# Products on 64 rows by turns between the two halves of the array, and selection operands filled up to 128 rows

## The chip, the cores and the metric

The kernel runs on one core of a Trainium2 chip, in one launch. The time is that of the device in microseconds, from launch to end; a comparison rests on the median of several runs. The profile is of one execution.

## The reference

A small language model with several kinds of layers is applied to one sequence of 256 tokens with 1024 channels, all in float32. Eleven stages follow each other: an RWKV-7 mixer, a gate with a per-layer embedding, differential attention, a second such gate, a norm, a feed-forward block, a Mamba-2 mixer (state space), two feed-forward blocks, sliding-window attention, and a last feed-forward block. Three of them contract over 64 elements only, and one over 64 selected rows:

```
# RWKV-7, 16 heads of 64, per token
sa    = einsum('bhij,bhj->bhi', state, kk_t)
state = state * w_t - sa b_t + v_t k_t ;  y_t = einsum('bhij,bhj->bhi', state, r_t)
...
# differential attention, 8 heads with two maps of 64 each
s   = einsum('bhcqd,bhckd->bhcqk', qi, kt) * scale        # c: the two maps
att = softmax(s)[:, :, 0] - lam * softmax(s)[:, :, 1]
...
# Mamba-2, 32 heads in 4 groups
seg    = acum[:, :, None] - acum[:, None, :]
scores = cb[..., None] * exp(where(causal, seg, -inf))
...
# sliding-window attention, 16 heads of 64 with 2 key heads
p = softmax(q k^T / 8 + bias, with a sink)
```

## The kernel before, in words

Tokens are held as two tiles of 128. Every product with weights is made of three products in a rounded float32 format (an upper and a lower part of each operand, the lower by lower one left out): `wload` fetches 512 KB of a weight matrix through SP's queue into `wr`, ScalarE makes the upper part `wh`, VectorE the lower part `wl`, and the sums stand in the long PSUM buffers `pl` (four banks). Everything else on TensorE writes into the short PSUM buffers `ps` (four banks; `pm`, `pq` and `pt` are one and the same).

Each stage is written as Python generators. `weave` runs them by turns, one step up to each `yield`; that order is the priority with which a scheduler then places the instructions on the engines, by its own estimate of when each is ready. `late` fixes an instruction behind what its engine was given earlier.

In the RWKV stage the 16 heads are four groups of four. A group runs through projections (`pre`), then for each of two chunks of 128 tokens through `scores` and `solve`, then `post`; the four groups start some turns after each other, and gate projections and others fill in between. `scores(t, g)` transposes the rows of two heads at a time, so that one head of a pair lies on partitions 0 to 63 and the other on 64 to 127 (`E_`). For each of the four heads it then takes one `ps` buffer, makes two products over 64 rows (128 x 256 each, plain float32, which the trace shows as two records each), and multiplies the result with a mask in two VectorE operations, into `GB` and `GK`. A `yield` follows each head. The inverse of a triangle (six levels of small float16 products, each into a `ps` buffer) and the delta rule come after it.

In differential attention `head(hd)` makes for each of its two maps one `ps` buffer with two products over 64 rows (128 x 128 and 128 x 256), then the softmax of this map, then a `yield`. Two chains of heads run beside each other. In sliding-window attention `front(pr)` does the same for the two heads of a pair.

In the state-space stage `heads(g)` needs, for each of 8 heads, the cumulated decays of that head on every partition. They come by a product of a selection matrix `sel` (64 rows, 8 x 128 columns) with the transposed decays `aT` (64 rows by 384 used columns; rows 32 to 63 hold the lower parts), in the rounded float32 format, one record each. Two small bfloat16 products add the causal mask. `sel` is a new tile for each of the four groups, with one buffer; two VectorE copies fill it. Before that, `aT` is written by one ScalarE and two VectorE operations.

Of the kernel before, what the change touches and what calls it, by code (L numbers as in the profile page):

```python
# [18 lines left out]
P = 128  # L19
D = 1024  # L20
NEG = -1.0e30
NREF = 1  # refinements of the triangular solve
# banks of PSUM for short and for long use
# [12 lines left out]
# columns of the constant block  # L36
# [3 lines left out]
def constants():  # L40
    """Masks, the identity, rotary angles and distance buckets: from the shapes alone."""
# [18 lines left out]
    # reversed distance vector: column m holds the distance 255 - m; row 32 the mask outside the window  # L60
# [14 lines left out]
def weave(*gens):  # L75
    """Trace the generators by turns, a step each."""
    gens = list(gens)
    while gens:
        for g in list(gens):
            try:  # L80
                next(g)
            except StopIteration:
                gens.remove(g)
# [13 lines left out]
def par(*gens):  # L97
    """The generators by turns, as one generator."""
    gens = list(gens)
    while gens:  # L100
        for g in list(gens):
            try:
                next(g)
            except StopIteration:
                gens.remove(g)
        yield


def spread(n, m, gen):
    """The generator's n steps over m turns."""  # L110
    at = 0
    for i in range(m):
        while at * m < (i + 1) * n:
            at += 1
            if next(gen, gen) is gen:
                return
        yield
    yield from gen


def spaced(n, *gens):
    """The generators one after another, n turns between."""
    for g in gens:
        yield from g
        for _ in range(n):
            yield


def when(cond, gen):
    """The generator, from the step on at which its condition holds."""  # L130
    while not cond():
        yield
    yield from gen
# [8 lines left out]
class Net:  # L142
# [27 lines left out]
    def m(self, shape, dt=F32, tag="m", bufs=24):  # L170
        """Small tiles: those without a tag outlive a stage, the others do not."""
        pool = self.mp if tag in ("m", "ecc", "bon", "junk") else self.st
        return pool.tile(list(shape), dt, tag=tag, name=self.nm(tag), bufs=bufs)
# [43 lines left out]
    def masked(self, out, a, b, least, init=3.0e38):  # L217
        """out = -(a + b), and its least element, not above init."""
        self.V.tensor_tensor_reduce(out=out, in0=a, in1=b, scale=-1.0, scalar=init, op0=ALU.add, op1=ALU.min,
                                    accum_out=least)  # L220
# [10 lines left out]
    def rsqrt(self, out, a, scale, eps):  # L231
        """out = (a * scale + eps) ** -0.5"""
# [4 lines left out]
    def bc(self, vec, n):  # L237
        """A DRAM vector on every partition."""
# [7 lines left out]
    def late(self, ins):  # L246
        """Not before what its engine was given earlier: for loads and constants that need not be early."""
        self.tc.keep_in_program_order(ins)

# [1 line left out]
    def prologue(self, cst):  # L251
# [10 lines left out]
        # short vectors, on every partition  # L262
# [11 lines left out]
    def first_cols(self, names, queue):  # L274
        """Per-channel vectors, channels onto partitions."""
# [16 lines left out]
    def load_x(self, tile, early=False):  # L292
        """The input, as the residual so far."""
# [18 lines left out]
    def more_cols(self):  # L312
# [14 lines left out]
        # the gain of the final norm and of the first feed-forward norm after it  # L327
# [9 lines left out]
    def wload(self, W, k0, kn, n0, nn):  # L337
        """[128, kn, nn] of W as an upper and a lower part that sum to it exactly."""
# [37 lines left out]
    def linear_cm_g(self, xT, K, W, n0, nn, evac):  # L376
        """The product with channels on partitions: evac takes two tiles of 128 channels by 256 tokens."""
# [16 lines left out]
    def linear2_g(self, xT, K, W, n0, evac):  # L394
        """256 columns, both token tiles side by side."""
# [22 lines left out]
    def split_g(self, src, ks, gains, outs):  # L418
        """src(t, k): [128 tokens, 128 channels]; appends channel-major pairs per gain."""
# [32 lines left out]
    def rstd(self):  # L452
        """Per-token 1/rms of the residual, [128, 2]."""
# [8 lines left out]
    def begin(self, gains):  # L462
        """The stage's input: per-token 1/rms and the residual, channel-major, times each gain."""
# [5 lines left out]
    def finish(self, l0, l1, gains):  # L469
        """The residual's two halves, and the next stage's input on the way."""  # L470
# [33 lines left out]
    def ffn(self, i, j, nxt, kv=False):  # L504
# [7 lines left out]
        def row():  # L512
            """1/rms as a row, on every partition."""
# [39 lines left out]
    def ple_proj(self, i):  # L553
        """p @ w_proj, kept in DRAM until its gate is known."""
# [35 lines left out]
    def final_norm(self):  # L590
        """The residual becomes its norm; what follows takes the operand from before it, the norm's
        gain and per-token factor folded in."""
# [13 lines left out]
    def rwkv(self, nxt):  # L606
        """The mixer up to its output projection: groups of four heads follow each other through
        projections, scores, triangular inverse, delta rule and group norm."""
# [22 lines left out]
        # normed input and its difference to the token before, channels on partitions  # L631
# [38 lines left out]
        def lora():  # L670
            """First stage of the low-rank decay (partitions 0-63) and in-context rate (64-127)."""
# [15 lines left out]
        def value(g):  # L687
            """Values less their mean over the head: the rule keeps the columns apart, so its output
            comes out centred as well."""
# [22 lines left out]
        def pre(g):  # L712
            """Decay and in-context rate, then keys and receptances, scaled by the running decay."""
# [68 lines left out]
        def scores(t, g):  # L782
            """One chunk of 128 tokens: products of the scaled rows, and the inverse (transposed,
            rounded) of the unit triangle that the delta rule solves with."""
# [11 lines left out]
            for hd in range(4):  # L796
                e, pr = E_(hd), hd // 2
                ps = self.pq()
                x = o[e, pr].rearrange("p a b -> p (a b)")
                self.mm(ps[:, 0:256], bk[e, pr, 0], x)  # L800
                self.mm(ps[:, 256:512], bk[e, pr, 1], x)
                for d, at in ((G, 0), (Gk, 256)):
                    self.mul(d[:, :, hd], t2(ps[:, at:at + 256]), mask)
# [43 lines left out]
        def solve(t, g):  # L847
            """The four heads' delta rule over the chunk, with the state before it and the state after."""
# [61 lines left out]
        def post(g):  # L910
            """Group norm (of rows centred already), bonus, gate."""
# [30 lines left out]
        def residual():  # L942
            """Loaded once the scan is well under way."""
# [13 lines left out]
    def diff(self, nxt):  # L957
# [5 lines left out]
        # lambda, on every partition  # L963
# [6 lines left out]
        self.stt(nlam[:], ls[:, 1:2], -LAM0, ls[:, 0:1], ALU.add, ALU.subtract)  # -(lambda)  # L970
        sub_row = self.vec["da_subln"]
        # rotary tables with the norm (and, for queries, the scale) folded in
# [47 lines left out]
        # the causal mask, after columns without one  # L1020
# [4 lines left out]
        def head(hd):  # L1025
# [3 lines left out]
            for c in range(2):  # L1029
                rs = slice(c * 64, c * 64 + 64)  # L1030
                ps = self.pq()
                self.mm(ps[:, 0:P], qT[rs, 0:P], kT[rs, 0:P])
                self.mm(ps[:, P:384], qT[rs, P:256], kT[rs, :])
# [53 lines left out]
    def ssm(self, nxt):  # L1087
# [6 lines left out]
        def conv(c0, ps, out):  # L1094
            """ps: two channel tiles [128, 2, 256]; twice the silu of the convolution into out."""
# [13 lines left out]
        def proj_cm(n0, done):  # L1109
            """512 columns; their convolution with channels on partitions."""  # L1110
# [17 lines left out]
        # step sizes: softplus(v) = max(v, 0) + 2 atanh(e / (2 + e)), e = exp(-|v|)  # L1128
# [10 lines left out]
        def steps():  # L1139
            # channels 0-31: with the weights' upper part, 32-63: with their lower part  # L1140
# [37 lines left out]
        # decays, twice side by side  # L1178
# [17 lines left out]
        aT = self.m([64, 512], F32R, "aT", 1)  # L1196
        self.act(aT[:, 0:256], pb[:64, 0:256])
        self.sub(aT[32:64, 0:256], pb[32:64, 0:256], aT[32:64, 0:256].bitcast(F32))
        self.V.tensor_copy(aT[:, 256:384], aT[:, 128:256].bitcast(F32))
        # 0.5 dt for the halves left out of the silu  # L1200
# [33 lines left out]
        def heads(g):  # L1234
# [5 lines left out]
            sel = self.m([64, 8, P], F32R, "sel", 1)  # L1240
# [40 lines left out]
        def piece(w):  # L1281
            """A piece of the work beside the heads, by its name."""
# [21 lines left out]
    def shared_kv(self, r, x):  # L1304
        I = self.I
        self.kT, self.kv, vv = {}, {}, self.s()
        kn = self.m([P, 64], tag="kn", bufs=1)  # the keys' gain, and the queries'
# [28 lines left out]
    def bias_vec(self):  # L1336
        """Per head, the bias against the distance (and the mask outside the window), to DRAM."""
# [12 lines left out]
    def swa(self, nxt):  # L1350
# [14 lines left out]
        def qproj(f):  # L1365
            qq, pss, ss = {}, [], self.m([P, 2, 8])

            def ev(t, ps):
                # with r inside the root: 1/8 of r rsqrt(r^2 sum / 64 + eps)
# [28 lines left out]
        def front(pr):  # L1398
            """Both heads' exponentials, and what divides them."""
            kv = pr // 4  # L1400
            for e_ in range(2):
                hd, rs = pr * 2 + e_, slice(e_ * 64, e_ * 64 + 64)
                ps = self.pq()
                self.mm(ps[:, 0:P], qT[pr][rs, 0:P], self.kT[rs, kv, 0:P])
                self.mm(ps[:, P:384], qT[pr][rs, P:256], self.kT[rs, kv, :])
# [64 lines left out]
    def gains(self, stage):  # L1470
        """Gains that the stage's input is taken with."""
# [80 lines left out]
```

## Time and profile before

| what | value |
|---|---|
| median of 3 runs | 1572.88 us (1570.53 to 1576.21) |
| span of the profiled execution, first to last instruction | 1568.3 us |
| own time of the profiled execution | not listed apart from the three runs; the median lies 4.6 us above the span |
| TensorE busy | 1525.5 us, 97% of the span |
| VectorE, ScalarE, GpSimd busy | 1065.5, 815.9, 77.5 us |
| mean granted TensorE clock | 0.997 of full speed |
| read from memory, written | 242.16 MB, 6.29 MB |

Instructions are counted as busy from start to modelled end, and TensorE's overlap; the distance from one start to the next start tells more of what one occupies. "s" and "ps" are names of tiles, `pl<-wh,s` means that `pl` is written from `wh` and `s`; `64*128` after MATMUL is rows by columns of the array, and `64x256` the operand that streams through. L226 is the helper `mm` and L197 the helper `tt`, so tiles tell where an instruction belongs: `qr,bk` are the scores of RWKV, `aT,sel` the selection, and `s,s` with 64 rows the attention maps and heads.

### The profile page before, as it was taken

How to read it: one execution, taken by the hardware profiler on the slowest of the kernel's cores; microseconds unless marked ns; L12 is line 12 of the kernel's file. 1: busy time of each engine (PE TensorE's matmuls, PEld its weight loads, DVE VectorE, ACT ScalarE, POOL GpSimd, SP SyncE). 2: the span in 40 equal slices, each digit the busy share in tenths (PEclk: the TensorE clock that was granted, in tenths of full speed). 3: DMA queues.
4: the chain of work that ended last, by engine and by line, in shares of the span. 5: the costliest groups of instructions: out<-in, count | busy, mean ns of one | idle time of the engine just before them, and what ended most of it. 6: DMA issues, size and time to landing. Idle time of an engine off the chain costs nothing.

```text
span 1568.3 us, 25792 instructions
## 1 busy us (share of the span) xinstructions
PE 1525.5 (97%) x10164; PEld 1349.5 (86%) x10164; DVE 1065.5 (68%) x1796; ACT 815.9 (52%) x1374; POOL 77.5 (5%) x79
## 2 busy tenths in 40 slices
PE   4999999999899999999999999999999999999998
PEld 4988988777678999887777899998999987799987
DVE  6887777876587756559877756665665657666563
ACT  3546546554466544447666744444544445654342
POOL 0000001111200000000000000000000002000000
PEclk9999999999999999999999999999999999999999
DMA  7421224566946554664442555465554653255463
GB/s 206 139 78 57 73 78 145 181 203 156 248 137 202 181 194 135 229 190 136 121 121 95 178 174 193 154 230 172 165 192 157 229 189 119 85 185 166 159 213 107
DMA packets 145500, 249.88 MB, mean 159 GB/s; under 512 B 11161, under 2 KB 42921, under 8 KB 145380
## 3 DMA queue, kind: packets, MB, share of 16 engines
q1 hardware_dynamic: 138420, 233.87, 46.4%
q0 software_dynamic: 3200, 10.81, 3.3%
q10 hardware_dynamic: 3760, 3.58, 0.9%
q8 instruction: 79, 1.29, 0.3%
q14 instruction: 41, 0.34, 0.1%
HBM read 242.16 MB, written 6.29 MB: 158 GB/s over the span
## 4 chain that ended last, share of the span: by engine, by line
PE 90%; DVE 4%; DMA 2%; ACT 2%; POOL 1%; issue 1%; ACTq 0%; POOLq 0%; DVEq 0%
PE pl L226 73%; PE ps L226 13%; PE ps L229 3%; DMA wr<-in_da_w_in_dram 1%; DVE wl L197 1%; DVE s L197 1%; DMA wa<-in_rw_w_dram 1%; DVE ac L209 1%; ACT s L223 0%; POOL s L993 0%; DVE s L209 0%; POOL m L234 0%; ACT h L223 0%; DMA wr<-in_rw_w_in_dram 0%; DMA base<-in_constants_dram 0%
## 5 line engine op out<-in xcount | busy, mean ns | idle before, releaser
L226 PE MATMUL pl<-wh,s 128*128 128x512 f32 (+1 forms) x2336 | 681.2, 370 | 6.2 <-ACT wh L223 3.2
L197 DVE TENSOR_TENSOR wl<-wr,wh 128x1024 fp32r<-128x1024 f32 (+1 forms) x460 | 528.5, 1173 | 123.0 <-ACT wh L223 121.7
L223 ACT ACTIVATE wh<-wr 128x1024 fp32r<-128x1024 f32 (+1 forms) x460 | 451.1, 1012 | 171.8 <-PE pl L226 103.3
L226 PE MATMUL pl<-s,wh 128*128 128x256 f32 x2816 | 509.1, 283 | 0.0
L226 PEld LDWEIGHTS pl<-wh,s 128*128 128x128 f32 x2336 | 422.3, 189 | 77.8 <-ACT wh L223 6.4
L226 PEld LDWEIGHTS pl<-s,wh 128*128 128x128 f32 x2816 | 439.5, 192 | 0.2
L226 PE MATMUL pl<-wl,s 128*128 128x512 f32 (+1 forms) x1168 | 430.2, 369 | 2.1 <-DVE wl L197 2.1
L226 PE MATMUL pl<-s,wl 128*128 128x256 f32 x1408 | 398.5, 283 | 0.0
L226 PEld LDWEIGHTS pl<-s,wl 128*128 128x128 f32 x1408 | 270.2, 192 | 0.0
L226 PEld LDWEIGHTS pl<-wl,s 128*128 128x128 f32 x1168 | 221.5, 190 | 36.0 <-DVE wl L197 3.3
L223 ACT ACTIVATE s<-s 128x512 f32<-128x512 f32 (+2 forms) x97 | 61.0, 629 | 209.7 <-DVE s L197 209.7
L197 DVE TENSOR_TENSOR s<-pl,s 128x512 f32<-128x512 f32 x44 | 30.4, 691 | 93.7 <-PE pl L226 93.7
L197 DVE TENSOR_TENSOR s<-pl,R 128x512 f32<-128x512 f32 x44 | 30.3, 691 | 82.8 <-PE pl L226 82.6
L234 POOL TENSOR_TENSOR m<-m,base 128x2 f32<-128x2 f32 (+2 forms) x25 | 24.2, 970 | 1006.9 <-DVE m L215 1006.9
L223 ACT ACTIVATE h<-ps 128x512 f16<-128x512 f32 x88 | 48.1, 600 | 36.9 <-PE ps L226 36.8
L223 ACT ACTIVATE s<-ps,base 128x256 fp32r<-128x256 f32 (+1 forms) x104 | 45.7, 471 | 25.0 <-PE ps L229 16.2
L209 DVE SCALAR_TENSOR_TENSOR s<-ps,base,s 128x256 fp32r<-128x256 f32 x96 | 43.6, 479 | 7.2 <-ACT s L223 6.1
L223 ACT ACTIVATE junk<-H 128x512 bf16<-128x512 f32 x40 | 25.1, 627 | 43.6 <-DVE H L209 29.2
L209 DVE SCALAR_TENSOR_TENSOR s<-s,s 128x512 f32<-128x512 f32 x56 | 38.4, 685 | 10.1 <-ACT s L223 9.4
L209 DVE SCALAR_TENSOR_TENSOR H<-pl,m,H 128x512 f32<-128x512 f32 x16 | 12.0, 751 | 47.1 <-PE pl L226 47.1
L226 PE MATMUL ps<-h,h 128*128 128x128 f16 x544 | 42.7, 220 | 1.3 <-ACT h L223 1.2
L226 PEld LDWEIGHTS <-h 128*128 128x128 f16 x576 | 34.9, 99 | 8.4 <-issue 4.8
(229 smaller groups left out, 1324.9 us busy)
## 6 DMA issues: line engine op xcount, KB each, us to landing
wr<-in_ffn_w_dram SPq DMA_DIRECT2D x248, 512.0 KB, 4.6
wr<-in_ssm_w_in_dram SPq DMA_DIRECT2D x40, 512.0 KB, 4.5
wr<-in_rw_w_in_dram SPq DMA_DIRECT2D x32, 512.0 KB, 4.7
wr<-in_da_w_in_dram SPq DMA_DIRECT2D x32, 512.0 KB, 4.7
wr<-in_pe_w_gate_dram SPq DMA_DIRECT2D x16, 512.0 KB, 4.3
wr<-in_ffn_w_dram SPq DMA_DIRECT2D x32, 256.0 KB, 3.1
wr<-in_ssm_w_out_dram SPq DMA_DIRECT2D x16, 512.0 KB, 3.8
wr<-in_rw_w_out_dram SPq DMA_DIRECT2D x8, 512.0 KB, 6.6
```

What stands on the lines that cost most here:

```text
L197: self.V.tensor_tensor(out=out, in0=a, in1=b, op=op)
L209: self.V.scalar_tensor_tensor(out=out, in0=a, scalar=sc, in1=b, op0=op0, op1=op1, **k)
L223: self.A.activation(out, a, f, **k)
L226: self.T.matmul(out, l, r, start=start, stop=stop)
L229: self.T.transpose(out, a, self.ident)
L234: self.G.tensor_tensor(out=out, in0=out, in1=self.mhalf[:, :out.free_size()].rearrange("p (a b) -> p a b", a=out.shape[1]) if len(out.shap ...
```

## The change

In `scores` the two heads of a pair are taken together: two `ps` buffers are taken at once, and the four products are issued by turns, first operand on partitions 0 to 63, then on 64 to 127, then the second operand of each. A `yield` follows, and then the four masks. The number of turns is the same. In `head` of differential attention and `front` of sliding-window attention both maps, or both heads, take their buffers together, and the products alternate between the halves in the same way; the softmax parts then follow one after the other as before. In the state-space stage `aT` and `sel` have 128 rows; rows 64 to 127 are set to zero once by two VectorE memsets in program order, and `sel` is one tile for all four groups. All other lines of the diff are comments.

```diff
-            for hd in range(4):
-                e, pr = E_(hd), hd // 2
-                ps = self.pq()
-                x = o[e, pr].rearrange("p a b -> p (a b)")
-                self.mm(ps[:, 0:256], bk[e, pr, 0], x)
-                self.mm(ps[:, 256:512], bk[e, pr, 1], x)
-                for d, at in ((G, 0), (Gk, 256)):
-                    self.mul(d[:, :, hd], t2(ps[:, at:at + 256]), mask)
+            for pr in range(2):
+
+                two = [self.pq(), self.pq()]
+                for a in range(2):
+                    for e, ps in enumerate(two):
+                        q = E_(e)
+                        self.mm(ps[:, a * 256:(a + 1) * 256], bk[q, pr, a], o[q, pr].rearrange("p a b -> p (a b)"))
+                yield
+                for e, ps in enumerate(two):
+                    for d, at in ((G, 0), (Gk, 256)):
+                        self.mul(d[:, :, pr * 2 + e], t2(ps[:, at:at + 256]), mask)
                 yield
...
-            for c in range(2):
-                rs = slice(c * 64, c * 64 + 64)
-                ps = self.pq()
-                self.mm(ps[:, 0:P], qT[rs, 0:P], kT[rs, 0:P])
-                self.mm(ps[:, P:384], qT[rs, P:256], kT[rs, :])
+            two = [self.pq(), self.pq()]
+            for q, ks in ((slice(0, P), slice(0, P)), (slice(P, 256), slice(0, 256))):
+                for c, ps in enumerate(two):
+                    rs = slice(c * 64, c * 64 + 64)
+                    self.mm(ps[:, q.start:q.start + ks.stop], qT[rs, q], kT[rs, ks])
+            for c, ps in enumerate(two):
                 S = e()
...
-        aT = self.m([64, 512], F32R, "aT", 1)
-        self.act(aT[:, 0:256], pb[:64, 0:256])
+
+        aT = self.m([P, 512], F32R, "aT", 1)
+        sel = self.m([P, 8, P], F32R, "sel", 1)
+        self.late(self.V.memset(aT[64:P, 0:384].bitcast(F32), 0.0))
+        self.late(self.V.memset(sel[64:P].bitcast(F32), 0.0))
+        self.act(aT[:64, 0:256], pb[:64, 0:256])
         self.sub(aT[32:64, 0:256], pb[32:64, 0:256], aT[32:64, 0:256].bitcast(F32))
-        self.V.tensor_copy(aT[:, 256:384], aT[:, 128:256].bitcast(F32))
+        self.V.tensor_copy(aT[:64, 256:384], aT[:64, 128:256].bitcast(F32))
...
-            sel = self.m([64, 8, P], F32R, "sel", 1)
...
-            for e_ in range(2):
-                hd, rs = pr * 2 + e_, slice(e_ * 64, e_ * 64 + 64)
-                ps = self.pq()
-                self.mm(ps[:, 0:P], qT[pr][rs, 0:P], self.kT[rs, kv, 0:P])
-                self.mm(ps[:, P:384], qT[pr][rs, P:256], self.kT[rs, kv, :])
+            two = [self.pq(), self.pq()]
+            for q, ks in ((slice(0, P), slice(0, P)), (slice(P, 256), slice(0, 256))):
+                for e_, ps in enumerate(two):
+                    rs = slice(e_ * 64, e_ * 64 + 64)
+                    self.mm(ps[:, q.start:q.start + ks.stop], qT[pr][rs, q], self.kT[rs, kv, ks])
+            for e_, ps in enumerate(two):
+                hd = pr * 2 + e_
                 S = e()
```

## Rows read from the trace of the kernel before

**Rows 1.** Page, the chain that ended last, shares by engine

```profile
PE 90%; DVE 4%; DMA 2%; ACT 2%; POOL 1%; issue 1%; ACTq 0%; POOLq 0%; DVEq 0%
```

**Rows 2.** Busy time by stretch: stretch, length, then each engine (instructions), clock, DMA

```profile
core 0: us, PE busy (x) PEld busy (x) DVE busy (x) ACT busy (x) POOL busy (x), PEclk, DMA share, GB/s
87.00:250.00 163.00, 161.67 (x1392) 140.86 (x1391) 125.76 (x240) 84.21 (x149) 10.21 (x7) 1.00 0.26 79
190.00:215.00 25.00, 25.00 (x218) 22.34 (x215) 23.07 (x44) 12.26 (x21) 0.00 (x0) 1.00 0.21 65
...
740.00:860.00 120.00, 119.09 (x660) 92.42 (x659) 96.56 (x167) 77.90 (x157) 4.44 (x4) 1.00 0.38 116
```

**Rows 3.** Waits of TensorE, 87 to 250: total us, times, longest

```profile
PE ps L226 <- DVE h L197: 0.7, 1, 0.7
```

**Rows 4.** TensorE's products by form: busy us, mean ns, idle before

```profile
L226 PE MATMUL ps<-qr,bk 64*128 64x256 f32 x128 | 33.7, 401 | 0.1
...
L226 PE MATMUL ps<-aT,sel 64*128 64x384 f32 x32 | 14.1, 440 | 0.0
```

**Rows 5.** Timeline of TensorE around one head's scores: start, length, what

```profile
98.14 1.13 PE L226 MATMUL ps<-qr,bk 64*128 64x256 f32 x4
99.19 0.38 PE L226 MATMUL pl<-wh,s 128*128 128x256 f32 x1
```

**Rows 6.** Timeline of TensorE, the scores of the first chunk

```profile
87.12 2.10 PE L226 MATMUL ps<-qr,bk 64*128 64x256 f32 x16
89.15 0.33 PE L229 MATMUL ps<-base,b 128*128 128x128 f32 x1
```

**Rows 7.** Timeline of TensorE, sliding window

```profile
1318.12 0.40 PE L226 MATMUL pl<-wh,s 128*128 128x512 f32 x1
1318.45 0.93 PE L226 MATMUL ps<-s,s 64*128 64x128 f32 x8
1319.31 0.50 PE L226 MATMUL pl<-wh,s 128*128 128x512 f32 x1
...
1319.88 0.40 PE L226 MATMUL pl<-wh,s 128*128 128x512 f32 x1
1320.20 0.92 PE L226 MATMUL ps<-s,s 64*128 64x128 f32 x4
1321.05 0.50 PE L226 MATMUL pl<-wh,s 128*128 128x512 f32 x1
```

**Rows 8.** Timeline of TensorE at full height (520 us) and around a selection (792 us)

```profile
520.00 0.28 PE L226 MATMUL pl<-s,wl 128*128 128x256 f32 x1
520.12 0.40 PE L226 MATMUL pl<-s,wh 128*128 128x256 f32 x2
...
791.88 0.40 PE L226 MATMUL pl<-wl,s 128*128 128x512 f32 x1
792.12 0.40 PE L226 MATMUL pl<-wh,s 128*128 128x512 f32 x1
792.44 0.44 PE L226 MATMUL ps<-aT,sel 64*128 64x384 f32 x1
792.81 0.28 PE L226 MATMUL ps<-sb 128*128 128x128 bf16 x2
```

**Rows 9.** VectorE's instructions by form: busy us, mean ns, idle before

```profile
L197 DVE TENSOR_TENSOR GB<-ps,hold 128x256 f32<-128x256 f32 x32 | 13.5, 421 | 11.7 <-PE ps L226 11.4
...
L936 DVE MEMSET S<- 128x1024 f32 x1 | 0.9, 912 | 0.2 <-issue 0.2
```

**Rows 10.** The chain that ended last, 395 to 420 us: start, length, what

```profile
399.29 17.86 DMA wr<-in_da_w_in_dram
```

**Rows 11.** Timeline of TensorE, maps of differential attention

```profile
434.46 2.34 PE L226 MATMUL ps<-s,s 64*128 64x128 f32 x16
436.73 0.50 PE L226 MATMUL pl<-wh,s 128*128 128x512 f32 x1
...
449.20 1.57 PE L226 MATMUL ps<-s,s 64*128 64x128 f32 x8
450.70 0.50 PE L226 MATMUL pl<-wl,s 128*128 128x512 f32 x1
```

## The prediction

> **What bounds the kernel now.** I read the chain that ended last first: TensorE holds 90% of it, so a time is won here only where TensorE's queue becomes shorter [rows 1]. Then the busy times by stretch, for the stages that hold 64-row products: in the RWKV scan (87 to 250 us) TensorE is busy 161.67 of 163 us, in the state-space stage (740 to 860) 119.09 of 120, while VectorE has 125.76 and 96.56 [rows 2]. The waits of TensorE say the same: over the whole scan the longest is 0.7 us [rows 3]. So in these stretches a product that leaves TensorE earlier moves everything behind it. Busy time can't tell what a product costs, since products overlap; I therefore price them by start to next start in the timeline.
>
> **What a stay on 64 rows costs.** There are 128 records of score products (a float32 product is two records) and 32 of the selection [rows 4]. A lone head's two score products, four records, start at 98.14, and the next product starts at 99.19: 1.05 us [rows 5]. In the first chunk all four heads come in one run, 16 records in 89.15 - 87.12 = 2.03 us [rows 6], half of 4 x 1.05. The sliding-window stage shows the reason in one view: eight records, both heads of a pair, take 1319.31 - 1318.45 = 0.86 us, and four records of one head 1321.05 - 1320.20 = 0.85 us [rows 7]. Products on the two halves of the rows run at the same time when they lie next to each other in the queue; a lone head leaves half of the array empty. The full-height product just before a stay also costs more: 1318.45 - 1318.12 = 0.33 and 1320.20 - 1319.88 = 0.32 us, where a 512-column product otherwise takes 792.12 - 791.88 = 0.24 [rows 7, 8]. That is 0.09 on entering.
>
> **Scores (RWKV).** The same products and masks remain; the two heads of a pair are issued by turns, with two PSUM buffers at once. Of 128 records 16 overlap already; the other 112 are 28 lone visits of 4, or 14 pairs. A pair now costs 2 x (1.05 + 0.09) = 2.28 us. Together, by the sliding-window pair, it should cost one visit: 1.05 + 0.01 + 0.09 = 1.15. Each pair saves 1.13 us, 14 pairs 15.8 us. Bounds: 0, if the two heads still lie apart in the queue, and 15.8. I take three quarters, 11.9: the scheduler has to find two of the four short PSUM buffers free together, and in between come the level products, which use the same four. VectorE sets a smaller limit: from 190 to 215 us it has 23.07 of 25 us [rows 2], so that stretch can give back 1.9 us, and two pairs in it would give 2.3. The four masks of a pair, some 0.42 us each [rows 9], are no more than before; they come a step after the products and lie behind other streams' VectorE work, which is hidden as long as TensorE has projection products to fill with.
>
> **Attention heads with two maps.** The first four heads' products fall ahead of a wait for weights: 17.86 us of the chain, from 399.29 us on, are a landing [rows 10]. What is saved just before it (two pairs of heads, at 0.7 to 1 us some 1.8) only makes that wait longer; I count nothing. Behind it, the run at 434.46 takes 436.73 - 434.46 = 2.27 us for two heads [rows 11]. Two pairs in a row would take 0.86 and then what a further pair adds: in the scan 2.03 - 1.05 = 0.98 for 4 records of 256 columns a head [rows 6], so for two of 128 and two of 256 columns three quarters, 0.73. That is 1.59: 0.68 saved. Heads 6 and 7 come as two lone visits (0.85 each, as in [rows 7]) and a run of 450.70 - 449.20 = 1.50 [rows 11], with three entries 3.47; as two visits of 0.95 they take 1.90, or 1.68 if they lie together: 1.6 to 1.8 saved. I take 2.2 of 2.3 to 2.5; bounds 0 and 4.3, the latter with the part ahead of the landing.
>
> **Sliding window.** Of eight pairs four overlap already. Two are lone visits: 2 x (0.85 + 0.09) against 0.95, 0.93 saved each. Two are cut differently and would save about 0.5 each. Together 2.9 us; I take 2.0, the two lone ones, and little of those that are cut differently, since such a cut can stay; bounds 0 and 2.9.
>
> **Selection operands filled to 128 rows.** The product keeps its 384 columns. Before: 792.44 - 792.12 = 0.32 for the product ahead of it (0.08 too much) and 792.81 - 792.44 = 0.37 for itself [rows 8]. At full height no trace shows it, but 384 columns lie between 256, which take 520.12 - 520.00 = 0.12, and 512, which take 0.24 [rows 8]: 0.12 to 0.24, I take 0.18, halfway as the columns are. Saved per product 0.08 + 0.37 - 0.18 = 0.27, over 32 products 8.6 us; bounds 32 x 0.21 = 6.7 and 32 x 0.33 = 10.6. Below that it would fall only if a 128-row product of this type were dearer than its 512-column neighbour, which nothing shows. Added once: two memsets on VectorE, in program order behind the cumulated decays. The nearest one, 128 x 1024, took 0.91 us [rows 9]; with the smaller one some 1.3 us. Queued behind them are the copies that make the operand and other channels' convolutions; projections cover it, and uncovered it costs 1.3. I take 0.3, so 8.3 net. That later groups now write into one lasting tile instead of a new one changes no wait: the copy waits for the group before either way.
> The Trainium skill, TensorE: Matmul & The Clock Gate, section Why this matters for your kernels, says that a product on few rows takes the time of a 128-row one and that only tiles running at once gain. By that sentence alone the filling would bring nothing, and the sum would be 16.1 us. [Rows 8] speak against it: the 384-column selection occupies 0.37 us where the 512-column product at full height takes 0.24.
>
> **Sum.** 11.9 + 2.2 + 2.0 + 8.3 = 24.4 us. The profiled execution spans 1568.3 us, so 1543.9 after; the median of the runs, 1572.88, lies 4.6 us above that span, which is taken as unchanged: 1548.5, rounded down to 1548. All upper values together give 15.8 + 4.3 + 2.9 + 10.6 = 33.6, or 1539.
>
> **Rivals.**
> 1. The pairs stay apart in the scan: the scheduler finds one short PSUM buffer, not two, and fills in other products between the heads. Then the scan saves 0, and 12.5 remains: 1560. For it: four buffers are shared by transposes, levels and scores. Against: in the first chunk four heads in a row found theirs [rows 6]. The Trainium skill, TensorEngine Tiling (Array Packing), Gotcha 1: PSUM Pressure, says that row tiles write to different banks and so raise the pressure on PSUM; the change does take two buffers at once, and the trace can't show yet whether they are there. Chance 0.14.
> 2. TensorE gets out of the way, and VectorE or the chain of levels becomes the limit: half of the scan and nothing in both attentions, 5.9 + 8.3 = 14.2, or 1559. For it: VectorE's 23.07 of 25 us; against: 125.76 of 163 over the whole scan [rows 2]. Chance 0.10.
> 3. The selection product occupies at full height what it does now, 0.37 us and 0.08 ahead of it [rows 8], because its rows were never what it paid for: then 24.4 - 8.3 = 16.1 us are saved, 1557. This is what the sentence of the Trainium skill above comes to. Chance 0.04.
> 4. The turns break up: each product finds its partner late and is issued alone. A visit then holds two records instead of four, and each additional visit costs about what the selection product's own costs above full height, 0.27. With 28 more in the scan and some 20 in the attentions 13 us are lost against 8.3 won: about 1578 at worst, 1572 with half of it; that is no change. Chance 0.06.
> 5. Slower: two short buffers are held from the first product to the last mask, and levels and transposes of the other groups wait for one at the head of TensorE's queue. There are 16 + 8 + 8 = 32 pairs. Four masks follow each other in about 1.3 us; if the whole of it stalled TensorE every time, 42 us would be lost against 24.4 won: 1590. The kernel is slower than before from 24.4 / 32 = 0.76 us of stall per pair on. Against: TensorE waits 0.7 us at most today [rows 3], and projection products stand ready. Chance 0.05.
>
> **How the numbers follow.** My forecast (most pairs together, selection at full rate) has 0.61, its own range being 1539 to 1556. With rivals 1, 2 and 3 the kernel is faster: 0.61 + 0.14 + 0.10 + 0.04 = 0.89, of which I give 0.02 to no change, since 12 us could still be lost in a new instruction order: 0.87. Within 0.3% (4.7 us, about what three runs between 1570.5 and 1576.2 can tell): 0.06 + 0.02 = 0.08. Slower 0.05. The range reaches from the upper sum less a microsecond of scatter, 1538, to rival 1 with 3 us of it, 1563.
>
> **What would show it.** Score records in runs of 8 with about 1.07 us from start to next start; selection rows with 128 rows and some 0.18 us to the next start, the product ahead of them at 0.24; the scan's end some 12 us and the state-space stage some 8 us shorter. Wrong would be: lone runs of 4 or of 2 records, TensorE waits for masks or buffers that add up to microseconds in the scan, or selection products that still take 0.37.

## The result and the profile after

The changed kernel takes 1552.87 us in the median (1551.96 to 1554.26, 4 runs) against 1572.8 before: a ratio of 0.9869, 95% interval 0.9854 to 0.9884, so 20.6 us (18 to 23) less; the two medians themselves lie 19.9 us apart. The profiled execution spans 1550.0 us, 18.3 less than before. Forecast were 1548 and a range from 1538 to 1563.

The same views as in [rows 2 to 8], of the changed kernel. To compare busy times, both kernels need stretches that hold the same work. ScalarE rounds 460 weight tiles in the same order in both, so the start of the k-th is a clock for both. Between tiles 10 and 40 lies the scan, between tiles 180 and 220 the heads of the state-space stage. The scan, first of the kernel before, then of the changed one (stretch, length, then each engine, clock, DMA); TensorE runs 1843 products in either:

```profile
52.10:268.20 216.10, 213.36 (x1843) 188.73 (x1842) 168.81 (x318) 115.29 (x203) 16.08 (x16) 1.00 0.29 90
53.60:257.90 204.30, 198.83 (x1843) 180.13 (x1842) 166.31 (x318) 114.24 (x203) 15.24 (x16) 1.00 0.30 95
```

The state-space heads in the same way:

```profile
709.70:878.60 168.90, 167.19 (x895) 132.24 (x894) 138.34 (x255) 116.76 (x224) 7.60 (x8) 1.00 0.39 119
699.90:861.50 161.60, 158.20 (x895) 131.31 (x894) 138.80 (x257) 115.57 (x224) 8.74 (x8) 1.00 0.42 124
```

So the scan is 11.8 us shorter: TensorE is busy 14.5 us less and stands idle 2.7 us longer. The state-space heads are 7.3 us shorter: 9.0 us less busy, 1.7 us more idle.

TensorE's products by form (busy us, mean ns, idle before) and its waits in the changed scan, up to 255 us (total, times, longest):

```profile
L226 PE MATMUL ps<-qr,bk 64*128 64x256 f32 x128 | 18.2, 400 | 0.0
...
L226 PE MATMUL ps<-aT,sel 128*128 128x384 f32 x32 | 11.7, 372 | 0.1
```

```profile
PE ps L226 <- ACT h L223: 2.8, 4, 1.4
PE ps L226 <- DVE GK L197: 1.3, 2, 1.1
PE ps L226 <- DVE sa L197: 0.6, 1, 0.6
PE ps L226 <- DVE h L197: 0.4, 1, 0.4
PE ps L226 <- ACT sa L223: 0.2, 1, 0.2
```

The score records keep one TensorE product or another running for 18.2 us in all instead of 33.7 [rows 4]: the mean of one is unchanged, so they lie on top of each other. The waits are now 5.3 us. In the kernel before they were 1.2 us up to 250 us, where [rows 3] end. But the same work goes on to 265 us there, and up to that point the waits were 2.4 us, half of them

```profile
PE ps L226 <- ACT h L223: 1.2, 2, 0.6
```

So 2.9 us of waits are new. The expectations below speak of 4 us; they set 5.3 against the 1.2 of the shorter stretch.

The timeline of TensorE (start, length, what) around one pair's scores, around a selection, and in the sliding window:

```profile
100.66 0.28 PE L226 MATMUL pl<-wl,s 128*128 128x256 f32 x1
100.87 1.14 PE L226 MATMUL ps<-qr,bk 64*128 64x256 f32 x8
101.94 0.62 PE L226 MATMUL ps<-h,h 128*128 128x128 f16 x8
...
779.43 0.39 PE L226 MATMUL pl<-wl,s 128*128 128x512 f32 x1
779.65 0.33 PE L226 MATMUL ps<-aT,sel 128*128 128x384 f32 x1
779.83 0.28 PE L226 MATMUL ps<-sb 128*128 128x128 bf16 x2
...
819.81 0.42 PE L226 MATMUL ps<-aT,sel 128*128 128x384 f32 x1
820.08 0.29 PE L226 MATMUL ps<-sb 128*128 128x128 bf16 x2
...
1302.75 0.40 PE L226 MATMUL pl<-wh,s 128*128 128x512 f32 x1
1303.08 0.93 PE L226 MATMUL ps<-s,s 64*128 64x128 f32 x8
1303.93 0.50 PE L226 MATMUL pl<-wh,s 128*128 128x512 f32 x1
```

Eight score records take 101.94 - 100.87 = 1.07 us to the next start, what four took before [rows 5]. All 16 pairs lie together: the stays add up to 17.2 us in 15 visits (the first holds two pairs), before to 31.7 us in 29. The selection's product takes 779.83 - 779.65 = 0.18 us to the next start behind a long product, and the product ahead of it 0.22, against 0.37 and 0.32 [rows 8]. Behind small products it takes 0.27 (820.08 - 819.81). Over all 32, product and the one ahead come to 12.7 us, before to 20.8.

Where the time went, stage by stage, by the clock of weight tiles; worked out from both traces, in us:

```
tile k     before    after    gained so far
10           52.1     53.6    -1.5   ahead of the scan (start-up)
40          268.2    257.9    10.3   behind the scan
70          369.7    359.3    10.4   ahead of differential attention's heads
100         486.2    476.4     9.7   behind them
180         709.7    699.9     9.8   ahead of the state-space heads
220         878.6    861.5    17.1   behind them
380        1311.6   1294.5    17.1   ahead of the sliding window's heads
459        1550.6   1532.4    18.3   last tile
```

So the scan gave 11.8 us, the state-space stage 7.3, the sliding window 1.2, and differential attention nothing (-0.7). The start-up, where the change has no part, went 1.5 us the other way in this execution; tile 10 starts between 52.1 and 55.7 us in the profiles of all kernels here.

### The profile page after: what moved, and what is told of

Read it like the earlier page. It is cut to its first block, busy times and chain, and to the rows that moved or that the text cites. A ratio compares the mean times of both kernels' runs of the same rounds, so it can differ in the third digit from the quotient of the medians.

```text
span 1550.0 us, 25809 instructions
## 1 busy us (share of the span) xinstructions
PE 1499.0 (97%) x10164; PEld 1336.5 (86%) x10164; DVE 1063.5 (69%) x1798; ACT 813.6 (52%) x1374; POOL 76.7 (5%) x79
## 4 chain that ended last, share of the span: by engine, by line
PE 85%; DVE 6%; DMA 3%; ACT 2%; POOL 2%; issue 1%; ACTq 0%; POOLq 0%; DVEq 0%
PE pl L226 71%; PE ps L226 10%; PE ps L229 3%; DVE wl L197 1%; DMA wr<-in_da_w_in_dram 1%; DVE s L197 1%; DMA wa<-in_rw_a_dram 1%; DVE s L209 1%; ACT wh L223 1%; ACT s L223 1%; POOL m L234 1%; DMA wr<-in_pe_w_gate_dram 0%; POOL m L1382 0%; ACT e L223 0%; DVE ac L209 0%
## 5 line engine op out<-in xcount | busy, mean ns | idle before, releaser
L226 PEld LDWEIGHTS pl<-wl,s 128*128 128x128 f32 x1168 | 221.7, 190 | 35.4 <-DVE wl L197 3.2
```

Source lines behind the costliest of these rows:

```text
L226: self.T.matmul(out, l, r, start=start, stop=stop)
```

## The experiments

**One part alone, three times.** The kernel before with the diff of the scores only, of the selection operands only, of both attentions only.

> The kernel before with the scores of the scan alone taken in pairs. My theory: every pair becomes one visit of 8 records of about 1.07 us, which takes some 15.6 us out of TensorE's queue, and about 4 us of it come back as waits of TensorE for masks and levels; so 11 to 13 us faster than before, near 1561. Rival 1 (the scan's gain is a matter of the scheduler's new order as a whole, not of the visits): anything from 0 to 20, and not the sum with the other parts. Rival 2 (all of the visits' time is won): 15 to 16 us, near 1557.

> The kernel before with the selection operands alone filled up to 128 rows. My theory: 0.2 to 0.27 us for each of 32 products, so 6.5 to 8.5 us faster, near 1565.5. Rival (a 128-row product costs as much as a 64-row one): no change, 1572 to 1574. With scores_only and attn_only the gains should add up to the 20 us of the whole change within 3 us.

> The kernel before with the products of both attentions alone by turns. My theory: the first four heads' part is swallowed by the landing of weights behind them, two heads later stay lone visits, and the sliding window gives about 1 us: 0 to 2 us faster, near 1572. Rival (the shorter visits count as they are, as the sum had it): 4 to 5 us faster, near 1568.5.

Measured: 1560.89 us for the scores, ratio 0.993 (0.9912 to 0.9947), 8 to 14 us less; 1567.75 for the selection, 0.9965 (0.9954 to 0.9977), 4 to 7 us less; 1571.02 for the attentions, 0.9985 (0.9977 to 0.9993), 1 to 4 us less. The three ratios multiply to 0.988, the whole change has 0.9869: the parts add up. The time of the scores matches the theory that 11 to 13 us of 15.6 come through, and is below the 15 to 16 of rival 2; but of the 4 us that the theory sends back as waits the profile shows less than half, 4.2 us of waits where the kernel before has 2.4. The selection lies at or below the lower end of what I expected, and the attentions reach above the 0 to 2 us of theirs. Part of this is TensorE's clock, in a stage that the selection does not touch: from 400 to 445 us its granted clock was 0.89 in the profile of the selection alone and 0.92 in that of the attentions alone, against 0.96 in that of the kernel before.

**Head by head.** The changed kernel, with the loops of the scores swapped:

```diff
-                for a in range(2):
-                    for e, ps in enumerate(two):
-                        q = E_(e)
+                for e, ps in enumerate(two):
+                    q = E_(e)
+                    for a in range(2):
```

> The changed kernel, but in the scores both buffers are taken together and the products go head by head: two on partitions 0 to 63, then two on 64 to 127. My theory: it is enough that the two heads lie next to each other in the queue; visits stay at 1.07 to 1.1 us and the time within 1.5 us of the changed kernel, near 1553. Rival (TensorE starts products strictly in their order, so only turns overlap): each of 16 visits takes 0.9 us more, 14 us slower than the changed kernel, near 1567.

Measured 1553.22 us, ratio to the kernel before 0.987 (0.9854 to 0.9885), the same as the changed kernel's. TensorE's timeline of this kernel around a pair:

```profile
101.86 0.28 PE L226 MATMUL pl<-wl,s 128*128 128x256 f32 x1
102.07 1.14 PE L226 MATMUL ps<-qr,bk 64*128 64x256 f32 x8
103.15 0.23 PE L226 MATMUL ps<-h,h 128*128 128x128 f16 x1
```

1.08 us for eight records, though both products of the first head are issued ahead of both of the second. The trace bears out that the order differs: the second head's first record starts 13 or 14 ns behind the first head's in 14 of the 15 visits, and 6 or 7 ns in 13 of 15 in the changed kernel. What gains is that the two heads lie next to each other; turns between the halves are not needed. The Trainium skill, TensorE: Matmul & The Clock Gate, section The mechanism, says that products start and end strictly in their order; by that this kernel's visits would have to be nearly twice as long, and the trace does not agree: 1.08 us.

**The selection twice.** The kernel before, with one line added ahead of the selection product, which writes over what it made:

```diff
+                self.mm(ps[:, 0:384], sel[:, q], aT[:, :384])
                 self.mm(ps[:, 0:384], sel[:, q], aT[:, :384], stop=False)
```

> The kernel before, and each of the 32 selection products (still on 64 rows) is made twice in a row into the same buffer; the result is the same. My theory: a visit on 64 rows costs a fixed amount on entering and leaving, and the second product in it only its columns, 0.16 to 0.18 us: 5 to 6 us slower than before, near 1579. Rival (a 64-row product in this format is itself dear, 0.37 us each): 11 to 12 us slower, near 1585.

Measured 1577.76 us, ratio 1.0026 (1.0016 to 1.0037), 2.5 to 6 us more, which contains the 5 to 6 of the theory and excludes the 11 to 12 of the rival. In the timeline a visit with two products lasts 755.13 - 754.59 = 0.54 us:

```profile
754.59 0.61 PE L226 MATMUL ps<-aT,sel 64*128 64x384 f32 x2
755.13 0.29 PE L226 MATMUL ps<-sb 128*128 128x128 bf16 x2
```

With one it lasted 0.37 [rows 8]. The second product costs 0.17 us, its columns, so the rest of the 0.37, some 0.2, is paid once per visit, and some 0.1 more by the product ahead. So the larger part is a cost of coming to 64 rows and leaving them, and not of each product on 64 rows. Both products of a visit load the same weights, each for itself (64 weight loads in the trace, 32 before).

**Masks at once.** The changed kernel, with the four masks of a pair traced in the step of its products (the first `yield` moved behind them).

> The changed kernel, but the four masks of a pair are traced in the same step as its products, and the two steps follow; the number of steps is the same. My theory: the 4 us of waits that the scan has gained come from masks that stand a step later behind other VectorE work, so TensorE's waits in the scan fall from 5.3 to 1 to 3 us and the time by 2 to 4 us, near 1550. Rival (the waits are those of the levels, which run into ScalarE and VectorE now that TensorE is shorter): within 1 us of the changed kernel, near 1553.

Measured 1556.14 us, ratio 0.9887 (0.9872 to 0.9903): 3 us above the changed kernel, with intervals that overlap, where 2 to 4 us below were expected. In the profile TensorE's waits in the scan came to 6.0 us instead of falling from 5.3 to 1 to 3, and those for masks grew from 1.3 to 3.0:

```profile
PE ps L226 <- DVE GK L197: 3.0, 4, 1.6
```

This profile is of the slowest of the four executions, 1560.05 us, with TensorE's granted clock at 0.53 from 140 to 151 us; but the fastest, 1554.90, is no gain either. The theory that the masks stand a step too late falls.

**Masks twice,** on both kernels: every mask is applied a second time into the same place. The changed kernel's VectorE time that the second expectation starts from stands in this row:

```profile
88.50:240.00 151.50, 148.26 (x1403) 133.48 (x1402) 124.71 (x243) 83.64 (x150) 9.37 (x7) 1.00 0.27 85
```

> The kernel before, and each of the 64 masks of the scores is made twice; the result is the same. VectorE gets some 64 x 0.33 = 21 us more in the scan, where it has 125.8 of 163 us. My theory (in the changed kernel VectorE, not TensorE alone, sets part of the scan): here most of it is hidden, 3 to 8 us slower than before, near 1578. Rival (what the scan did not win is lost in the order of levels and has nothing to do with how much VectorE does): see the next kernel.

> The changed kernel with the same doubled masks. VectorE would have 124.7 + 21 of 151.5 us. My theory: it is slower than the changed kernel by at least 3 us more than masks_twice_before is slower than before, so 8 to 14 us, 1561 to 1567. Rival: the same loss as on the kernel before within 2 us.

Measured 1593.75 us on the kernel before, ratio 1.0125 (1.0108 to 1.0142), 20 us more; and 1565.48 on the changed one, which is 12.6 us more than 1552.87. That is the reverse of what I expected: the changed kernel lost less. A part of both is TensorE's clock: at the start of the scan its granted clock (the column behind the engines) was 0.86 in the kernel before with doubled masks and 0.95 in the changed one, against 1.00 in [rows 2]:

```profile
87.00:120.00 33.00, 28.30 (x183) 22.43 (x182) 26.46 (x60) 10.71 (x18) 1.95 (x1) 0.86 0.25 67
87.00:120.00 33.00, 28.36 (x223) 24.16 (x222) 29.57 (x64) 12.48 (x20) 1.64 (x1) 0.95 0.30 87
```

So this pair does not decide how much VectorE limits each kernel. Some 21 us of added VectorE work, with the slower clock that came with it, cost 20 and 12.6 us, although [rows 3] have TensorE waiting for next to nothing.

**Half of the masks.** The changed kernel without the mask on the second half of each score, which ScalarE copies instead.

```diff
-                    for d, at in ((G, 0), (Gk, 256)):
-                        self.mul(d[:, :, pr * 2 + e], t2(ps[:, at:at + 256]), mask)
+                    self.mul(G[:, :, pr * 2 + e], t2(ps[:, 0:256]), mask)
+                    self.act(Gk[:, :, pr * 2 + e], t2(ps[:, 256:512]))
```

> The changed kernel, but the mask on the second half of each score (GK) is left out, and ScalarE copies that half instead: part of the computation is missing. VectorE loses 32 x 0.33 = 10.6 us in the scan, ScalarE gains some 15 and stays below TensorE. Theory 1 (VectorE's share is what keeps the scan from the 4 us that the shorter visits should still give): TensorE's waits in the scan fall to 1 to 3 us and the time by 3 to 5 us, near 1549. Theory 2 (the waits are those of a chain from product to mask to product, whichever engine does the middle): within 1.5 us of the changed kernel, 1551.5 to 1554.5.

Measured 1554.95 us, ratio 0.9888 (0.9871 to 0.9904): not faster than the changed kernel, and 0.5 us above the range of theory 2. Busy times of its scan, again from weight tile 10 to 40, and TensorE's longest waits there:

```profile
53.30:260.50 207.20, 200.31 (x1845) 180.60 (x1843) 156.76 (x286) 123.60 (x236) 16.16 (x16) 1.00 0.30 94
```

```profile
PE ps L226 <- DVE h L197: 1.5, 2, 1.3
PE ps L226 <- DVE sa L197: 1.4, 3, 0.6
PE ps L226 <- ACT GK L223: 1.4, 1, 1.4
```

VectorE has 9.6 us less to do than in the changed kernel (166.31), ScalarE 9.4 us more, and TensorE waits about as long as before (5.8 us), now for the copy on ScalarE and for results further down. So moving this much work off VectorE does not shorten the waits. What less VectorE work would do without new copies on ScalarE, this run does not show.

**The write of the bias vectors elsewhere.** `bias_vec` (3 MB written through GpSimd's queue) is called at the start of the state-space stage instead of in differential attention, in the kernel before and in the changed one; and, for the changed one, just ahead of the state-space heads.

> The kernel before, with the bias vectors of the sliding window (3 MB written to memory through GpSimd's queue) moved from the middle of differential attention to the start of the state-space stage. My theory: this write is what holds up the weights at 399 to 417 us, so the landing leaves the chain there and the kernel is 5 to 9 us faster than before, near 1566, unless the state-space stage pays for it. Rival (the weights wait for their buffers, not for the write): no change.

> The changed kernel with the same move. My theory: without the landing the shorter visits of the first four attention heads count as well, so this kernel stands 1 to 3 us further below bias_later_before than the changed one stands below the one before, that is 21 to 23 us, near 1544. Rival (that part is lost in the softmax chain, landing or not): 20 us or less below it.

> The changed kernel with the write of the bias vectors moved to where the heads of the state-space stage begin, which ask for 117 GB/s of weights instead of the some 200 of differential attention. My theory: the landing leaves the chain in differential attention, 5 to 7 us, and the heads lose less than bias_later's start of that stage did (7 to 8 us): 1546 to 1550. Rival (the write holds up weights wherever it stands): 1550 to 1554.

Measured 1574.54 us on the kernel before, ratio 1.001 (1.0001 to 1.0019), and 1550.28 on the changed one, 0.9857 (0.9843 to 0.9871): 24 us apart, where 21 to 23 were expected; but neither kernel came near its forecast of 1566 and 1544 us. The write is what holds up the weights of [rows 10]: from 372 to 420 us a load of 512 KB took 14.4 us in the median to land in the kernel before, and 4.2 us with the write moved away (KB each, us to landing):

```profile
wr<-in_da_w_in_dram SPq DMA_DIRECT2D x12, 512.0 KB, 14.4
scr<-s POOLq DMA_DIRECT2D x1, 3072.0 KB, 35.5
...
wr<-in_da_w_in_dram SPq DMA_DIRECT2D x12, 512.0 KB, 4.2
```

By the clock of weight tiles 7.0 us are won between tiles 70 and 90. But TensorE then waits at the start of the state-space stage, and all of it is given back there:

```profile
PE ps L229 <- ACT s L223: 5.0, 1, 5.0
PE pl L226 <- DVE wl L197: 2.7, 2, 1.6
```

The landing has only moved: the write is issued at 698.2 us and lands 35.4 us later, and in the chain that ended last stands a weight load that was issued behind it and landed with its end:

```profile
707.75 25.29 DMA wr<-in_ssm_w_in_dram
```

The write holds up weights in each of the three places; in the third a load issued at 723.9 us took 25.5 us. Without the landing differential attention gives 0.7 us between the two moved kernels (11.8 ahead of the heads, 12.5 behind them), where -0.7 stood with it. That is the direction of the theory, but no more than this stage differs between profiles of kernels that have it alike (115.2 to 117.7 us in five profiles with the changed attention and the write in its old place). The other microseconds that the pair gains arise elsewhere: 9.5 us in the state-space stage instead of 7.3, 12.7 in the scan instead of 11.8. Half of this theory stands, the write as the cause of the landing, and half stays unproven. The third place gave 1572.52 us, ratio 0.9981 (0.9962 to 1.0), 20 us slower than the changed kernel and far above both forecasts; the last section shows where this went.

None of these beats the changed kernel beyond the intervals; bias_later_after, 2.6 us lower, overlaps with it.

## Why the prediction was right, step by step

By part, forecast and found in the profile: scores 11.9 and 11.8 us, selection 8.3 and 7.3, sliding window 2.0 and 1.2, differential attention 2.2 and -0.7.

**TensorE's queue sets the time.** Right: what left its queue in the scan and the state-space stage came out of the time for the most part. But a queue without waits is not a queue with room behind it. The scan's waits were 2.4 us before and 5.3 after; the chain that ended last went from 90% TensorE [rows 1] to 85%:

```profile
PE 85%; DVE 6%; DMA 3%; ACT 2%; POOL 2%; issue 1%; ACTq 0%; POOLq 0%; DVEq 0%
```

**Scores.** The size of a joined visit (1.07 us, 1.15 with its entry) was right, and so was the result, 11.9 us forecast and 11.8 measured, but that it fits so well is luck. I took three quarters because I doubted that two short buffers would be free together. They always were: all pairs joined, which takes 31.7 - 17.2 = 14.5 us from the stays. TensorE's busy time in the scan fell by just that, 213.36 - 198.83 = 14.5; the 14 entries of 0.09 that the sum adds to it do not show in the total. Then 2.7 us came back as idle time, so that 11.8 are left. How much comes back differs from profile to profile: scores_only and bias_later_after, whose scans hold the same products, wait 4.2 us instead of 5.3. What exactly sets these waits stays open: having the masks sooner did not remove them, nor did having fewer of them on VectorE with copies on ScalarE in their place. A chain from product to mask to level to product is what is left, and no run shows it.

**Turns.** The prediction laid the gain to lying next to each other; head_by_head shows it, and that the turns themselves add nothing.

**Selection.** 0.27 us each, 8.6 in all, were forecast for TensorE's queue; by product and entry it is 20.8 - 12.7 = 8.1, and the busy time of the stage fell by 9.0. The time gained 4 to 7 us alone and 7.3 in the changed kernel's profile, not 8.3, because 1.7 us of idle time are new, most of it one wait of 1.6 us at 775 us for a multiplication of a head's scores on VectorE. I had charged 0.3 for two memsets instead. These took 0.91 and 0.38 us, the 1.3 I had worked out from [rows 9], and ended by 716 us; no run shows that they cost any time.

**Differential attention.** This term was wrong: 2.2 us forecast, none seen in the profile of the changed kernel. TensorE's busy time from tile 70 to 100 did fall, from 109.66 to 107.98 us, but its idle time grew from 6.8 to 9.1. In head_by_head, with the same attention, the same stage took 115.4 us, 1.1 less than before, and 117.1 in the changed kernel, so a gain of about a microsecond is not excluded. The run of [rows 11] did shrink from 2.27 to 1.57 us. Heads 6 and 7 did not do as assumed: of their four maps two stayed lone visits, and only the last two joined. Each lone visit holds both products of one map, so the queue does not keep the order in which the change issues them:

```profile
436.60 0.92 PE L226 MATMUL ps<-s,s 64*128 64x128 f32 x4
437.45 0.50 PE L226 MATMUL pl<-wl,s 128*128 128x512 f32 x1
437.88 0.92 PE L226 MATMUL ps<-s,s 64*128 64x128 f32 x4
438.73 0.73 PE L226 MATMUL pl<-wh,s 128*128 128x512 f32 x2
439.39 0.93 PE L226 MATMUL ps<-s,s 64*128 64x128 f32 x8
440.25 0.50 PE L226 MATMUL pl<-wl,s 128*128 128x512 f32 x1
```

That leaves 0.7 + 0.6 us of shorter visits behind the landing, and they do not reach the end of the stage. The part ahead of the landing gave nothing, as forecast; the landing's piece of the chain is as long as before, 18.30 us from 388.02 on against 17.86 [rows 10].

**Sliding window.** 2.0 forecast, 1.2 measured. The two lone pairs joined (1.9 us); of the two that were cut differently one was cut worse, and the stays fell from 9.4 to 8.4 us with two entries less.

**Rivals.** Buffers kept no pair apart (rival 1), no turn broke up in the scan (4), and no stall of 0.76 us a pair arose (5). Rival 2, that something other than TensorE limits, is true for about a fifth of what left TensorE's queue in the scan, 2.7 of 14.5 us.

## What to carry to other kernels

Look for products on few rows among others at full height and price the visit, not the product: here a visit of one selection product to 64 rows cost 0.2 to 0.3 us on top of its columns, so filling the operands with zeros paid although the columns stayed the same. Two heads on the two halves took in one visit what one took alone, and for that it was enough that both stood next to each other in the queue, in either order. And not all that leaves a full queue comes out of the time, even if that queue waits for nothing today: in the scan and in the state-space stage here about four fifths did (11.8 of 14.5 us, 7.3 of 9.0), in differential attention, which stands behind a landing, none for certain. Compare stretches that hold the same work: a window that ends a little earlier in one kernel made 2.9 us of new waits look like 4.1.

## What the runs showed of the hardware that I had not expected

A lone visit costs as much as a visit of both halves to within 0.01 us (0.85 and 0.86 in [rows 7]), and the overlap does not need the instructions to alternate: 1.08 us head by head, 1.07 by turns.

A lower granted clock came with longer waits, in a stretch and not as a state of the whole run. In bias_in_heads_after the state-space heads (weight tiles 180 to 220) take 188.0 us, 26.4 more than in the changed kernel, where these are the 161.6 us shown with the result:

```profile
694.10:882.10 188.00, 172.49 (x890) 141.53 (x889) 140.78 (x260) 116.15 (x224) 12.72 (x11) 0.90 0.53 138
732.00:743.00 11.00, 4.16 (x12) 3.30 (x13) 3.08 (x6) 2.78 (x6) 0.00 (x0) 0.53 0.98 155
831.00:856.00 25.00, 24.07 (x94) 20.48 (x95) 12.51 (x20) 9.70 (x24) 0.00 (x0) 0.52 0.14 43
```

TensorE stands idle 15.5 us in this stage instead of 3.4, most of it in two waits:

```profile
PE ps L229 <- DVE s L209: 11.0, 2, 9.2
```

And it is busy 14.3 us longer with the same work. The granted clock was near half of full speed in two pieces, that is, for nearly all of them at 1.2 instead of 2.4 GHz: from 732 to 743 us, in which the wait of 9.2 us ended, and from 831 to 856 us, where TensorE was busy for 24.07 of 25 us after it had stood idle for 0.5 and 1.5 us around 830. TensorE was busy for 28.2 us in the two pieces; at full clock that work would by estimate have taken half, some 14 us less. So the 26 us are about half waits and half clock; 8.4 us won in differential attention and 3.0 lost in the scan make up most of the rest of what this kernel lost. The runs do not show what decides when the clock falls: in the changed kernel a wait of 1.6 us in the same stage left it at 1.00.
